# Host-side weight tiles with 8 KB rows, and stored activation sums loaded into a free quarter of a weight buffer

## The chip, the cores and the metric

The kernel runs on one core of a Trainium2 chip. The metric is device time in microseconds (us), lower is better. Engines are named as in the profile: PE is TensorE, DVE is VectorE, ACT is ScalarE, POOL is GpSimd, SP is the sync engine, whose queue issues nearly all DMAs here.

## The reference

One encoder block on a sequence of 256 tokens of width 2048, all in float32:

```python
hn = rmsnorm(h, mix_norm_pre)
proj = hn @ w_in                       # 2048 x 4640: z 1024, xbc 1536, dt 32 and u 1024
y_ssd = ssd_mixer(z, xbc, dt_raw, ...)  # bidirectional Mamba-2 scan
y_pool = pool_mixer(u, pool_w, pool_scale)
mix = concatenate([y_ssd, y_pool]) @ w_out            # 2048 x 2048
h = h + rmsnorm(mix, mix_norm_post)
hn = rmsnorm(h, ffn_norm_pre)
ff = conv_glu(hn, w_ffn_up, ..., w_ffn_down)          # 2048 x 11264, then 5632 x 2048
h = h + rmsnorm(ff, ffn_norm_post)
gate = sigmoid(rmsnorm(h, ple_norm_pre) @ w_ple_gate)  # 2048 x 2048
out = h + rmsnorm(gate * (p @ w_ple), ple_norm_post)   # 256 x 2048
```

## The kernel before

Nearly all the time is matrix products of the 256 tokens with weights that are read from HBM once. To keep float32 accuracy, every operand is split into a high part in a reduced format and a low part, the rest. Each product is then three products: high by high, high by low, low by high. The split of a weight tile is one cast on ACT (names ending in `whi`) and one subtraction on DVE (names ending in `wlo`); it is the function `split`.

Weights come through four buffers of 128 x 2048 float32 (8 KB in each of 128 partitions, 1 MB), all under the tag `raw`; a load takes the next buffer in turn and must wait until the last reader of that buffer is done. SP issues the loads in program order, so a load that waits holds those behind it. The split parts go into five buffers of `whi` and five of `wlo`. Smaller tiles come from a pool of five `mid` buffers. The order of the instructions on each engine is set by the kernel's scheduler, which works from the program and a model of durations.

Four functions load weights. `feature_major` (columns xbc of `w_in`) reads 4 row blocks of 128 x 512, so rows of 2 KB. `feature_pairs` (the up-projection, loads named ug and uv, outputs ga and va) reads 8 blocks of 128 x 256, rows of 1 KB. `token_major` (z, output projection wo, down-projection dn, gate gt, ple) reads two blocks of 128 x 1024, rows of 4 KB, by `pair_of_rows`. A first loop reads the dt and u columns of `w_in` (loads dtur), 128 x 1056 at a time.

In the down-projection the 5632 hidden columns are taken in 22 pairs of 128, and the output columns in two halves of 1024. For 10 of the 22 pairs in the first half and 11 in the second (the list `seven`) the product of 2 x 2 blocks is made with seven products instead of eight (`seven_products`). Such a fast block needs sums of weight quarters (`weight_sums`) and sums of activations. The activation sums are made during the up-projection and stored in HBM, 256 KB for each pair (`block_sums`). `hid_sums` loads them again into a `mid` tile, one block ahead of their use, and splits them into a tile `hs`. The weight sums of 7 pairs are made ahead too, in both halves of the columns, and stored (`block_ahead`); their 14 fast blocks load the sums as one 1 MB tile, `bm`, and of the weights themselves only three quarters, by `three_blocks`, in two pieces: a quarter and a half. The first quarter of that `raw` buffer stays unused. The tiles of a fast block carry its row number: block 5 of the first half is dn010, block 6 is dn012. The output projection has three fast blocks, two of which come through `three_blocks`; their activation sums never leave the chip.

Of the kernel before, what the change touches and what calls it, by code (L numbers as in the profile page):

```python
# [50 lines left out]

def build(nc, a, out):
    x = a["x"][0]
    w_in, w_out, w_up = a["w_in"][0], a["w_out"][0], a["w_ffn_up"][0]
    w_down, w_gate, w_ple = a["w_ffn_down"][0], a["w_ple_gate"][0], a["w_ple"][0]
    out = out[0]

    with tile.TileContext(nc) as tc, \
# [34 lines left out]
        ident = cp.tile([P, P], F32, name="ident")  # L93
        make_identity(nc, ident)

        c_dt = DSSD + 1536
        r0 = wp.tile([P, 2048], F32, tag="raw", bufs=4, name="dtur0")
        for n in range(2):
            first = ins(nc.scalar.dma_start(r0[:, n * 352:(n + 1) * 352],
                                            w_in[:P, c_dt + n * 352:c_dt + (n + 1) * 352]))  # L100

        with tc.issue_after(first):
            nc.scalar.activation(tiny("tables", 1), mhalf[:, 0:1], AF.Exp)
# [32 lines left out]
            return xt[0][:, i:i + 1] if i < V_SCW else vt[:, i - V_SCW:i - V_SCW + 1]  # L136


        spare, ready, held = {}, {}, {}

        def parts(name):

# [16 lines left out]
            last["dma"] = load(r[:, :a_ * b_].rearrange("p (a b) -> p a b", a=a_), src, True)  # L159
            return r  # L160

        def three_blocks(name, w, k0, c0):

            r = wp.tile([P, 2048], F32, tag="raw", bufs=4, name=name)
            load(r[:, 512:1024], w[k0 * P:(k0 + 1) * P, c0 + 512:c0 + 1024], True)
            last["dma"] = load(r[:, 1024:], w[(k0 + 1) * P:(k0 + 2) * P, c0:c0 + 1024], True)
            return r

        class Panel:
# [85 lines left out]
            add(acc[1][1], acc[1][1], s167)  # L255

        def pair_of_rows(w, k0, c0):
            return w[k0 * P:(k0 + 2) * P, c0:c0 + 1024].rearrange("(k p) c -> p k c", p=P), 2, 1024

        def split_two(name, w, k0, c0):  # L260

# [3 lines left out]
        def token_major(name, w, c0, ks, get, acc, tail=1, fast=(), alt=None, sums=None, hooks={}, made=None):  # L265


            group, nu, sums_of = [], len(ks) // 2, {}
            for u in range(nu):
                k0 = ks[2 * u]  # L270
                if u + 1 in fast:
                    sums_of[u + 1] = sums(ks[2 * u + 2])
                if u in fast:
                    sets = made(u, c0)
                    r = three_blocks(f"{name}r{k0}", w, k0, c0) if sets else raw(f"{name}r{k0}", *pair_of_rows(w, k0, c0))
                else:
                    two = ready.pop(name) if u == 0 and name in ready else split_two(name, w, k0, c0)
                if u in hooks:
                    hooks[u]()
                if u in fast:  # L280
                    seven_products(f"{name}{k0}", r, sums_of.pop(u)(), acc, alt, u == fast[0], u == fast[-1],
                                   sets and sets())
                    continue
                group.extend(two)
                if nu - tail <= u < nu - 1:
                    continue

                order = [(t, o, g, q) for t in range(2) for o in columns(acc[t]) for g in group for q in range(3)] \
                    if u == nu - 1 or u - 1 in fast[-1:] else \
                    [(t, o, g, q) for g in group for t in range(2) for q in range(3) for o in columns(acc[t])]  # L290
                for t, (o, c), (k, wh, wl), q in order:
                    xh, xl = (v[:, t * P:(t + 1) * P] for v in get(k))
                    xx, ww = ((xh, wh), (xh, wl), (xl, wh))[q]
                    mm(o, xx, ww[:, c:c + o.shape[-1]], k == ks[0] and q == 0, k == ks[-1] and q == 2)
                if u - 1 in fast[-1:]:
                    combine(name, acc, alt)
                group = []
                aside()

        def feature_major(name, w, c0, get, acc):  # L300

            for u in range(4):
                r = raw(f"{name}r{u}", w[u * 512:(u + 1) * 512, c0:c0 + 512]
                        .rearrange("(k p) c -> p k c", p=P), 4, 512)
                tiles = []

                def step(j, kk, f):
                    k = 4 * u + 2 * j + kk
                    (wh, wl), (xh, xl) = tiles[j], get(k)
                    s = slice(kk * 512 + f * P, kk * 512 + (f + 1) * P)  # L310
                    for q, (ww, xx) in enumerate(((wh, xh), (wh, xl), (wl, xh))):
                        mm(acc[f // 2][:, f % 2 * L:(f % 2 + 1) * L], ww[:, s], xx,
                           k == 0 and q == 0 and f % 2 == 0, k == NK - 1 and q == 2)
# [12 lines left out]
                aside()  # L326

        def feature_pairs(name, w, c0, get, acc):


            def high(u, tiles):
                for j, (wh, _) in enumerate(tiles):
                    for k, f, s in block(u, j):
                        mm(acc[f], wh[:, s], get.both(k), k == 0, False)

            def low(u, tiles):
                for j, (_, wl) in enumerate(tiles):
# [123 lines left out]
        for u in range(0, NK, 2):  # L461
            r = [wp.tile([P, 2048], F32, tag="raw", bufs=4, name=f"dtur{u}") if u else r0, page(f"dtur{u + 1}")]
            for j in range(2):
                k = u + j
                if k == 0:
                    last["dma"] = load(r[0][:, 704:1056], w_in[:P, c_dt + 704:c_dt + 1056])
                    xload(1, 2)
                    x_panel(1, 2)
                    continue
                for c0, c1 in ((0, 704), (704, 1056)) if k == 1 else ((0, 1056),):  # L470
                    last["dma"] = load(r[j][:, c0:c1], w_in[k * P:(k + 1) * P, c_dt + c0:c_dt + c1])
                if k == 1:
                    xload(2, 4)
                elif k in (3, 5, 7):
# [196 lines left out]

        def xbc(slab):
            acc = main(f"xbc{slab}")
            feature_major(f"xb{slab}", w_in, DSSD + slab * 512, hn, acc)
# [90 lines left out]
            [job(mix, 1, 1)],  # L765
        ])
        zacc = [main(f"z{t}") for t in range(2)]
        token_major("z", w_in, 0, list(range(NK)), hn, zacc)
        assert not work


# [56 lines left out]
        def cat_blocks(k):  # L828
# [108 lines left out]
        sums = {u: dp.tile([P, 512], F32, name=f"sums{u}") for u in seven}  # L937
# [21 lines left out]
        def block_sums(u, x):  # L959

            s = mid(f"hs{u}")
            activation_sums(s, x)
            stores.append(lambda: nc.sync.dma_start(sums[u], s[:, :512]))

        def store():
            for st in stores:
# [134 lines left out]
def laid_out(a):  # L1101

    def cols(*vs):
        return np.concatenate([v.reshape(-1, P).T for v in vs], axis=1)

    return {
        "x_cols": np.concatenate([cols(a["mix_norm_pre"][0]),
                                  a["x"][0].T.reshape(NK, P, L).transpose(1, 0, 2).reshape(P, NK * L)], axis=1),
        "p_t": a["p"][0, 0].T.reshape(2, P, L).transpose(1, 0, 2),
# [40 lines left out]
```

## Time and profile before

| | |
|---|---|
| three runs | 1117.62, 1118.17, 1120.74 us; median 1118.17 |
| profiled execution | 1116.37 us; its span is 1114.6 us |
| granted TensorE clock | 0.998 |
| PE / DVE / ACT busy | 99% / 75% / 61% of the span |
| DMA | 275.69 MB, mean 247 GB/s |

"Span" is the time from the first to the last instruction in the profiled execution. "Busy" shares are means over the span. The start of a row in a timeline is in us from the span's start, the next number is its length. A row of the list of waits reads: who waited, for whom, total us, times, longest. In a name, `<-` stands between what is written and what is read; `L87` is line 87 of the kernel.

### The profile page before, as it was taken

The page shows a single profiled execution, that of the slowest core. Times are in us where ns is not written, and L with a number is a line of the kernel's source. Part 1 is how long each engine was busy: PE and PEld are TensorE (multiplying, and loading weights), DVE is VectorE, ACT ScalarE, POOL GpSimd, SP SyncE. Part 2 cuts the span into 40 slices and gives each one's busy share as a digit, 9 for nine tenths or more (in the row PEclk, how much of TensorE's full clock was granted, in tenths as well). Part 3 has the DMA queues.
Part 4 walks back from the last instruction along what each step waited for, and adds up shares of the span by engine and source line. Part 5 has one row for each costly group of instructions (what it writes and reads, how often), then busy time and mean ns, then how long its engine had stood idle before and what let it go on. Part 6 is the DMA issues. An engine that isn't in the chain of part 4 may idle for free.

```text
span 1114.6 us, 15714 instructions
## 1 busy us (share of the span) xinstructions
PE 1102.6 (99%) x6040; PEld 964.0 (86%) x6040; DVE 834.2 (75%) x1047; ACT 683.7 (61%) x1006; POOL 53.0 (5%) x80
## 2 busy tenths in 40 slices
PE   9999999999999999999999999999999999999996
PEld 9999988888788888888888888888888888887885
DVE  6668888879786866767767777676888787897574
ACT  6757876555775565565655655556666466657462
POOL 0300023100200000000000000000000000001001
PEclk9999999999999999999999999999999999999999
DMA  9954445766587977877887797676888789886732
GB/s 354 375 175 150 154 151 186 262 215 224 213 283 252 302 264 247 272 268 255 270 296 254 241 323 255 211 254 205 279 293 303 255 285 314 307 283 214 247 132 76
DMA packets 145739, 275.69 MB, mean 247 GB/s; under 512 B 5504, under 2 KB 98560, under 8 KB 142208
## 3 DMA queue, kind: packets, MB, share of 16 engines
q1 hardware_dynamic: 145376, 274.33, 73.3%
q8 instruction: 47, 0.77, 0.3%
q10 hardware_dynamic: 288, 0.36, 0.1%
q14 instruction: 28, 0.23, 0.1%
HBM read 251.86 MB, written 22.81 MB: 246 GB/s over the span
## 4 chain that ended last, share of the span: by engine, by line
PE 92%; DMA 3%; ACT 2%; issue 1%; DVE 1%; POOL 0%; SPq 0%; DVEq 0%; POOLq 0%; ACTq 0%
PE va L87 22%; PE ga L87 21%; PE dna L87 15%; PE gt L87 7%; PE woa L87 7%; PE xbc L87 6%; PE dns L87 5%; PE z L87 4%; DMA dtur<-w_in 2%; DMA x<-x 1%; PE wos L87 1%; PE yd L87 1%; PE pw L87 1%; PE ple L87 0%; PE seg L87 0%
## 5 line engine op out<-in xcount | busy, mean ns | idle before, releaser
L87 PE MATMUL ga<-wox,ug_0whi 128*128 128x512 f32 x352 | 87.8, 391 | 0.0
L87 PE MATMUL va<-wox,uv_0whi 128*128 128x512 f32 x352 | 87.6, 391 | 0.0
L87 PE MATMUL ga<-wox,ug_1whi 128*128 128x512 f32 x352 | 87.2, 389 | 0.0
L87 PE MATMUL va<-wox,uv_1whi 128*128 128x512 f32 x352 | 86.9, 389 | 0.0
L87 PEld LDWEIGHTS va<-wox,uv_1whi 128*128 128x128 f32 x352 | 66.1, 188 | 13.7
L87 PEld LDWEIGHTS ga<-wox,ug_1whi 128*128 128x128 f32 x352 | 66.0, 188 | 13.7
L87 PEld LDWEIGHTS va<-wox,uv_0whi 128*128 128x128 f32 x352 | 64.6, 188 | 12.5
L87 PEld LDWEIGHTS ga<-wox,ug_0whi 128*128 128x128 f32 x352 | 64.6, 188 | 12.4
L87 PE MATMUL ga<-wox,ug_1wlo 128*128 128x256 f32 x352 | 49.7, 283 | 0.9 <-DVE ug_1wlo L153 0.9
L87 PE MATMUL ga<-wox,ug_0wlo 128*128 128x256 f32 x352 | 49.5, 283 | 0.0
L87 PE MATMUL va<-wox,uv_1wlo 128*128 128x256 f32 x352 | 49.4, 283 | 0.0
L87 PE MATMUL va<-wox,uv_0wlo 128*128 128x256 f32 x352 | 49.2, 283 | 0.0
L87 PEld LDWEIGHTS ga<-wox,ug_0wlo 128*128 128x128 f32 x352 | 46.8, 191 | 1.8
L87 PEld LDWEIGHTS va<-wox,uv_0wlo 128*128 128x128 f32 x352 | 46.7, 191 | 1.7
L87 PEld LDWEIGHTS ga<-wox,ug_1wlo 128*128 128x128 f32 x352 | 45.4, 192 | 1.3 <-DVE ug_1wlo L153 1.3
L87 PEld LDWEIGHTS va<-wox,uv_1wlo 128*128 128x128 f32 x352 | 45.4, 192 | 0.0
L875 POOL TENSOR_SCALAR dnm<-dnq,fmean 128x1 f32<-128x1 f32 x2 | 0.6, 282 | 586.8 <-ACT dnj L872 586.8
L87 PE MATMUL xbc<-hnh,xb_0whi 128*128 128x256 f32 x96 | 27.6, 288 | 0.3 <-ACT u L539 0.3
L87 PE MATMUL xbc<-hnh,xb_1whi 128*128 128x256 f32 x96 | 27.3, 285 | 0.0
L87 PE MATMUL xbc<-hnl,xb_1whi 128*128 128x256 f32 x96 | 27.2, 283 | 0.0
L87 PE MATMUL xbc<-hnh,xb_1wlo 128*128 128x256 f32 x96 | 27.1, 283 | 0.0
L87 PE MATMUL xbc<-hnh,xb_0wlo 128*128 128x256 f32 x96 | 27.1, 283 | 0.0
(1664 smaller groups left out, 3095.6 us busy)
## 6 DMA issues: line engine op xcount, KB each, us to landing
dn0r<-w_ffn_down SPq DMA_DIRECT2D x15, 1024.0 KB, 6.2
dn1r<-w_ffn_down SPq DMA_DIRECT2D x15, 1024.0 KB, 6.9
br<-w_ffn_down SPq DMA_DIRECT2D x14, 1024.0 KB, 5.5
bm<-block SPq DMA_DIRECT2D x14, 1024.0 KB, 5.0
zr<-w_in SPq DMA_DIRECT2D x8, 1024.0 KB, 5.3
wo0r<-w_out SPq DMA_DIRECT2D x8, 1024.0 KB, 5.8
gt0r<-w_ple_gate SPq DMA_DIRECT2D x8, 1024.0 KB, 5.9
gt1r<-w_ple_gate SPq DMA_DIRECT2D x8, 1024.0 KB, 5.5
```

Source lines behind the costliest of these rows:

```text
L87: last["pe"] = ins(nc.tensor.matmul(o, lhsT, rhs, start=start, stop=stop, skip_group_check=True))
L875: nc.gpsimd.tensor_scalar(m, q, 1.0 / D, mean[t], op0=ALU.mult, op1=ALU.add)
```

## The change

The host cuts each weight matrix into the kernel's own tiles before the launch, so that every 1 MB load is one contiguous block with a row of 8 KB in each partition. `w_in` is given as three arrays: z, xbc, and dt with u (there only the row blocks become contiguous, with rows of 4224 bytes as before). In the fast blocks with stored weight sums, the three quarters of weights come in one load instead of two. In the 14 such blocks of the down-projection the stored activation sums are loaded into the first quarter of the same `raw` buffer instead of into a `mid` tile; the 7 other fast blocks keep the old way. The casts and subtractions stay the same in number and size.

```diff
-        def three_blocks(name, w, k0, c0):
+        def three_blocks(name, w, k0, c0, rest=None):
             r = wp.tile([P, 2048], F32, tag="raw", bufs=4, name=name)
-            load(r[:, 512:1024], w[k0 * P:(k0 + 1) * P, c0 + 512:c0 + 1024], True)
-            last["dma"] = load(r[:, 1024:], w[(k0 + 1) * P:(k0 + 2) * P, c0:c0 + 1024], True)
+            if rest is not None:
+                load(r[:, :512], rest, True)
+            last["dma"] = load(r[:, 512:], w[c0 // 1024, k0 // 2][:, 512:], True)
             return r
...
         def pair_of_rows(w, k0, c0):
-            return w[k0 * P:(k0 + 2) * P, c0:c0 + 1024].rearrange("(k p) c -> p k c", p=P), 2, 1024
+            return w[c0 // 1024, k0 // 2].unsqueeze(1), 1, 2048
...
-                if u + 1 in fast:
+                if u + 1 in fast and not made(u + 1, c0):
                     sums_of[u + 1] = sums(ks[2 * u + 2])
                 if u in fast:
                     sets = made(u, c0)
-                    r = three_blocks(f"{name}r{k0}", w, k0, c0) if sets else raw(f"{name}r{k0}", *pair_of_rows(w, k0, c0))
+                    if sets:
+                        r = three_blocks(f"{name}r{k0}", w, k0, c0, stored.get(u) if name[:2] == "dn" else None)
+                        sums_of[u] = sums(k0, r)
+                    else:
+                        r = raw(f"{name}r{k0}", *pair_of_rows(w, k0, c0))
...
-                r = raw(f"{name}r{u}", w[u * 512:(u + 1) * 512, c0:c0 + 512]
-                        .rearrange("(k p) c -> p k c", p=P), 4, 512)
+                r = raw(f"{name}r{u}", w[c0 // 128 + u].unsqueeze(1), 1, 2048)
...
-                r = raw(f"{name}r{u}", w[u * 1024:(u + 1) * 1024, c0:c0 + 256]
-                        .rearrange("(k p) c -> p k c", p=P), 8, 256)
+                r = raw(f"{name}r{u}", w[c0 // 256, u].unsqueeze(1), 1, 2048)
...
-        def hid_sums(k):
-            s = mid(f"sums{k}")
-            load(s[:, :512], sums[k // 2], True)
+        def hid_sums(k, s=None):
+            if s is None:
+                s = mid(f"sums{k}")
+                load(s[:, :512], stored[k // 2], True)
...
+    def tiles(w, kt, n):
+        k, c = w.shape
+        return w.reshape(k // (kt * P), kt, P, c // n, n).transpose(3, 0, 2, 1, 4).reshape(c // n, k // (kt * P), P, kt * n)
...
+        "w_z": tiles(w_in[:, :DSSD], 2, 1024),
+        "w_xb": tiles(w_in[:, DSSD:DSSD + 1536], 4, 512).reshape(12, P, 2048),
+        "w_dtu": w_in[:, DSSD + 1536:].reshape(NK, P, 1056),
+        "w_out": tiles(a["w_out"][0], 2, 1024),
+        "w_ffn_up": tiles(a["w_ffn_up"][0], 8, 256),
+        "w_ffn_down": tiles(a["w_ffn_down"][0], 2, 1024),
```

The order of PE's instructions is the same but for six of them. The orders on SP, ACT and DVE move in the down-projection. SP's queue around the blocks 5 and 6 of the first half, before (`dn0r` is a `raw` buffer; `sums<-sums` loads stored activation sums into a `mid` tile; `bm` is the stored weight sums):

```order
L119 DMA sums_7690<-sums_3039 128x512
L119 DMA dn0r_7728<-w_ffn_down 128x512
L119 DMA dn0r_7728<-w_ffn_down 128x1024
L119 DMA bm_0_7734<-block_0_3050 128x2048
L119 DMA sums_7726<-sums_3040 128x512
L119 DMA dn0r_7773<-w_ffn_down 128x512
L119 DMA dn0r_7773<-w_ffn_down 128x1024
```

and after:

```order
L118 DMA dn0r_7720<-sums_3037 128x512
L118 DMA dn0r_7720<-w_ffn_down 128x1536
L118 DMA bm_0_7726<-block_0_3048 128x2048
L118 DMA dn0r_7765<-sums_3038 128x512
L118 DMA dn0r_7765<-w_ffn_down 128x1536
```

The sums of a block stood ahead of its weight buffer's turn, in a tile of their own; now they are the first thing loaded into that buffer. ACT's casts at the same place, before (`dn06` is block 3, whose sums are in a `mid` tile in both kernels; `hs` is the split of the activation sums; `dn_0` and `dn_1` are the plain block 4):

```order
L152 CAST dn06awhi<-dn0r_7643 128x512
L152 CAST dn06cwhi<-dn06f 128x1024
L152 CAST hs_7731<-sums_7690 128x512
L152 CAST dn06dwhi<-dn06g 128x1024
L152 CAST hs_7776<-sums_7726 128x512
L152 CAST dn_0whi<-dn0r_7692 128x1024
```

and after:

```order
L151 CAST dn06bwhi<-dn0r_7639 128x1024
L151 CAST hs_7723<-dn0r_7720 128x512
L151 CAST dn06awhi<-dn0r_7639 128x512
L151 CAST dn06cwhi<-dn06f 128x1024
L151 CAST dn06dwhi<-dn06g 128x1024
L151 CAST hs_7768<-dn0r_7765 128x512
L151 CAST dn_0whi<-dn0r_7686 128x1024
```

The cast of block 5's sums moved two places up, ahead of dn06awhi; that of block 6 stays ahead of dn_0whi and reads the new buffer.

More of the change, by code (lines that the diff above doesn't have):

```diff
@@ L53, in build @@
     x = a["x"][0]
-    w_in, w_out, w_up = a["w_in"][0], a["w_out"][0], a["w_ffn_up"][0]
-    w_down, w_gate, w_ple = a["w_ffn_down"][0], a["w_ple_gate"][0], a["w_ple"][0]
+    w_out, w_up, w_down, w_gate, w_ple = (a[n] for n in ("w_out", "w_ffn_up", "w_ffn_down", "w_ple_gate", "w_ple"))
+    w_dtu, w_xb, w_z = a["w_dtu"], a["w_xb"], a["w_z"]
     out = out[0]
@@ L94, in build @@
         make_identity(nc, ident)
-        c_dt = DSSD + 1536
         r0 = wp.tile([P, 2048], F32, tag="raw", bufs=4, name="dtur0")
@@ L99, in build @@
             first = ins(nc.scalar.dma_start(r0[:, n * 352:(n + 1) * 352],
-                                            w_in[:P, c_dt + n * 352:c_dt + (n + 1) * 352]))
+                                            w_dtu[0][:, n * 352:(n + 1) * 352]))
         with tc.issue_after(first):
@@ L136, in vec @@
             return xt[0][:, i:i + 1] if i < V_SCW else vt[:, i - V_SCW:i - V_SCW + 1]
-        spare, ready, held = {}, {}, {}
+        spare, ready, held, stored = {}, {}, {}, {}
         def parts(name):
@@ L465, in build @@
                 if k == 0:
-                    last["dma"] = load(r[0][:, 704:1056], w_in[:P, c_dt + 704:c_dt + 1056])
+                    last["dma"] = load(r[0][:, 704:1056], w_dtu[0][:, 704:1056])
                     xload(1, 2)
@@ L470, in build @@
                 for c0, c1 in ((0, 704), (704, 1056)) if k == 1 else ((0, 1056),):
-                    last["dma"] = load(r[j][:, c0:c1], w_in[k * P:(k + 1) * P, c_dt + c0:c_dt + c1])
+                    last["dma"] = load(r[j][:, c0:c1], w_dtu[k][:, c0:c1])
                 if k == 1:
@@ L673, in xbc @@
             acc = main(f"xbc{slab}")
-            feature_major(f"xb{slab}", w_in, DSSD + slab * 512, hn, acc)
+            feature_major(f"xb{slab}", w_xb, slab * 512, hn, acc)
             sc = times_rows(f"xr{slab}", acc, rxb)
@@ L767, in build @@
         zacc = [main(f"z{t}") for t in range(2)]
-        token_major("z", w_in, 0, list(range(NK)), hn, zacc)
+        token_major("z", w_z, 0, list(range(NK)), hn, zacc)
         assert not work
@@ L826, in cat_sums, with cat_blocks @@
             split([cat_s[n][:, c] for n in ("h", "l")], v[:, 512:], 0, 512)
-        def cat_blocks(k):
+        def cat_blocks(k, r=None):
             u = wo_ks.index(k) // 2
@@ L936, in build @@
         seven = [u for u in range(1, 19) if u % 5 in (0, 1, 3)]
-        sums = {u: dp.tile([P, 512], F32, name=f"sums{u}") for u in seven}
+        stored.update({u: dp.tile([P, 512], F32, name=f"sums{u}") for u in seven})
         ahead = [(u, half) for u in seven if u % 5 != 3 for half in range(2)]
@@ L962, in block_sums @@
             activation_sums(s, x)
-            stores.append(lambda: nc.sync.dma_start(sums[u], s[:, :512]))
+            stores.append(lambda: nc.sync.dma_start(stored[u], s[:, :512]))
         def store():
@@ L1104, in cols @@
         return np.concatenate([v.reshape(-1, P).T for v in vs], axis=1)
+    def tiles(w, kt, n):
+        k, c = w.shape
+        return w.reshape(k // (kt * P), kt, P, c // n, n).transpose(3, 0, 2, 1, 4).reshape(c // n, k // (kt * P), P, kt * n)
+    w_in = a["w_in"][0]
     return {
+        "w_z": tiles(w_in[:, :DSSD], 2, 1024),
[4 more added lines that the diff above has]
+        "w_ffn_down": tiles(a["w_ffn_down"][0], 2, 1024),
+        "w_ple_gate": tiles(a["w_ple_gate"][0], 2, 1024),
+        "w_ple": tiles(a["w_ple"][0], 2, 1024),
         "x_cols": np.concatenate([cols(a["mix_norm_pre"][0]),
@@ L1140 @@
     arrays.update(constants())
-    for n in ("p", "mix_norm_pre", "ssd_conv_w", "ssd_conv_b", "ssd_norm", "pool_scale", "ffn_norm_pre",
+    for n in ("p", "w_in", "mix_norm_pre", "ssd_conv_w", "ssd_conv_b", "ssd_norm", "pool_scale", "ffn_norm_pre",
               "ffn_conv_w", "ple_norm_pre", "ffn_conv_b", "ssd_dt_bias", "ssd_a_log", "ssd_d"):
```

## The prediction

> **What bounds the kernel now.** I read the busy shares first, then what TensorE (PE) waits for, then stretches of the span with their DMA share, then the chain. From the page's first and second parts:
>
> ```profile
> PE 1102.6 (99%) x6040; PEld 964.0 (86%) x6040; DVE 834.2 (75%) x1047; ACT 683.7 (61%) x1006; POOL 53.0 (5%) x80
> DMA packets 145739, 275.69 MB, mean 247 GB/s; under 512 B 5504, under 2 KB 98560, under 8 KB 142208
> ```
>
> PE is busy 99%, but its ends are modelled, so a wait can hide inside "busy". The view of waits, for PE alone, is complete in five rows:
>
> ```profile
> PE dtu L108 <- POOL ident masks.py:199: 1.4, 1, 1.4
> PE ga L87 <- DVE ug_1wlo L153: 0.9, 1, 0.9
> PE xbc L87 <- ACT u L539: 0.3, 1, 0.3
> PE dnxt L381 <- DVE h_back L886: 0.3, 1, 0.3
> PE woxt L381 <- DVE h L886: 0.3, 1, 0.3
> ```
>
> Not one of them ends on a load of weights: the first is the warm-up, the other four (1.8 us together) end on VectorE or ScalarE where one stage hands over to the next. Now the two stages that carry most of the loads, the up-projection and the down-projection, with three shorter stretches (columns: stretch and length, PE, PEld, DVE, ACT, POOL busy, clock, DMA share, GB/s):
>
> ```profile
> 303.30:782.80 479.50, 479.50 (x2765) 424.86 (x2766) 345.75 (x429) 281.75 (x419) 3.00 (x3) 1.00 0.80 262
> 782.80:1006.50 223.70, 223.70 (x989) 185.23 (x988) 184.89 (x195) 138.82 (x165) 1.70 (x7) 1.00 0.85 289
> 432.00:459.00 27.00, 27.00 (x161) 24.08 (x160) 18.51 (x22) 15.16 (x26) 0.00 (x0) 1.00 0.67 217
> 459.00:486.00 27.00, 27.00 (x150) 23.63 (x150) 21.19 (x29) 14.73 (x20) 0.00 (x0) 1.00 1.01 325
> 27.00:54.00 27.00, 26.68 (x170) 26.48 (x169) 17.38 (x22) 21.39 (x29) 9.89 (x10) 1.00 1.04 381
> ```
>
> The DMA engines are full in some stretches and a third idle in others, at the full clock, so the question is whether PE feels it. The chain says no:
>
> ```profile
> 427.22 22.23 PE ga L87 x128
> 449.45 22.23 PE va L87 x128
> 471.68 22.23 PE ga L87 x128
> ```
>
> One block of 128 matmuls takes 22.23 us at a DMA share of 0.67 and the same 22.23 us at 1.01. The next starts at the hundredth where the last ended. PE runs its own list of instructions at a fixed rate; loads only have to be there in time. DMA is busy but is not the bound.
>
> **The change, part by part.**
>
> (1) Longer rows. The loads by row size, as they are now (columns: name, count, size, median us from issue to landing):
>
> ```profile
> ug40r<-w_ffn_up SPq DMA_DIRECT2D x2, 1024.0 KB, 6.1
> xb0r<-w_in SPq DMA_DIRECT2D x4, 1024.0 KB, 5.0
> zr<-w_in SPq DMA_DIRECT2D x8, 1024.0 KB, 5.3
> bm<-block SPq DMA_DIRECT2D x14, 1024.0 KB, 5.0
> ug30r<-w_ffn_up SPq DMA_DIRECT2D x2, 1024.0 KB, 5.1
> uv40r<-w_ffn_up SPq DMA_DIRECT2D x2, 1024.0 KB, 10.5
> ```
>
> The first four have rows of 1, 2, 4 and 8 KB, and bm already has the new form: one contiguous tile. 1 MB lands in 5.0 us with 2 KB rows and with 8 KB rows alike; with 1 KB rows it lands in 5.1 us at best and in 10.5 where the stores and reloads of the same stage are in its way (the last two rows). As for throughput, the up-projection moves 262 / 0.80 = 328 GB/s per full DMA share with mostly 1 KB rows, the stretch 27 to 54 moves 381 / 1.04 = 366 with mostly 4 to 8 KB rows. So I estimate that the share of 0.80 falls to about 0.80 x 328 / 366 = 0.72. On the path this is worth nothing, since PE waits for no load. What hides it: the 479.5 us of PE. If that cover were gone, the 0.08 would be 38 us; that is a rival below.
>
> The Trainium skill, "DMA: Bandwidth & Descriptors", section "Why small descriptors are slow (HBM only)", gives a fixed overhead of about 3 cycles per packet against beats of 32 B; worked out from it, an estimate, a 1 KB row costs 35/32 and an 8 KB row 259/256, so 7.5% less DMA time. By that alone the share would be 0.74 and not 0.72; neither changes the sum, but if loads set the pace it would be worth 29 us.
>
> (2) The input projection's rows of 4224 B keep their size and only lie closer together. The start is where PE could feel them. PE's first real matmuls, from the timeline:
>
> ```profile
> 4.93 0.96 PE L87 MATMUL dtu<-dtu0whi,hnh 128*128 128x352 f32 x2
> 8.21 0.48 PE L87 MATMUL dtu<-dtu0whi,hnl 128*128 128x352 f32 x2
> 8.53 0.48 PE L87 MATMUL dtu<-dtu0wlo,hnh 128*128 128x352 f32 x2
> ```
>
> A pair takes 0.32 us once running (8.21 to 8.53). The last row is the ninth pair, so eight pairs took 3.60 us where 2.56 would do: 1.0 us of hidden waiting. The bound is a gain of 1.0 if all of it is the loads, a loss of the same size if landings get that much later; I take 0, because the row size, which is what the DMA engines see, stays.
>
> (3) Fewer issues. Each of the 16 fast blocks with stored weight sums (14 in the down-projection, 2 in the output projection) now takes one load of three quarters instead of two pieces, so 16 issues go from SP's queue. SP waits for buffers most of the time; nothing is gained on the path.
>
> (4) Stored sums into the weight buffer's free quarter, for 14 of the 21 blocks. This is the one place that can hurt, so I work it out at the first pair (blocks 5 and 6, tiles dn010 and dn012). Before, these loads go into their own tile; now each must wait until a weight buffer comes free. SP's issues (L119), ScalarE's casts and VectorE's subtractions there:
>
> ```profile
> 788.71 0.82 SPq L119 DMA_DIRECT2D dn0r<-w_ffn_down  x2
> 792.73 0.38 SPq L119 DMA_DIRECT2D sums<-sums  x1
> 794.05 0.82 SPq L119 DMA_DIRECT2D dn0r<-w_ffn_down  x2
> 790.69 1.05 ACT L152 CAST dn06bwhi<-dn0r 128x1024 fp32r<-128x1024 f32 x1
> 791.73 0.62 ACT L152 CAST dn06awhi<-dn0r 128x512 fp32r<-128x512 f32 x1
> 798.08 0.62 ACT L152 CAST hs<-sums 128x512 fp32r<-128x512 f32 x1 [1.08 <-DMA sums<-sums]
> 798.61 1.05 ACT L152 CAST dn_0whi<-dn0r 128x1024 fp32r<-128x1024 f32 x1
> 793.33 0.69 DVE L153 TENSOR_TENSOR dn06awlo<-dn0r,dn06awhi 128x512 fp32r<-128x512 f32 x1
> 799.69 1.23 DVE L153 TENSOR_TENSOR dn_0wlo<-dn0r,dn_0whi 128x1024 fp32r<-128x1024 f32 x1 [0.26 <-ACT dn_0whi L152]
> 803.09 0.62 PE L87 MATMUL dna<-dn_0whi,hidh 128*128 128x512 f32 x2
> 803.54 0.61 PE L87 MATMUL dna<-dn_0wlo,hidh 128*128 128x512 f32 x2
> ```
>
> and the landings that price it:
>
> ```profile
> dn0r<-w_ffn_down SPq DMA_DIRECT2D x7, 256.0 KB, 4.3
> sums<-sums SPq DMA_DIRECT2D x21, 256.0 KB, 5.4
> ```
>
> The buffer of block 5 is free at 788.71, so its sums go out then. They land 4.3 later at 793.0 (the 256 KB piece that today goes first into that very buffer takes 4.3). In the new order ScalarE's cast of these sums stands between dn06bwhi and dn06awhi. ScalarE, done with dn06bwhi at 791.74, waits until 793.0; the cast ends 0.62 later, dn06awhi at about 794.2, and dn06awlo at 794.9 instead of 794.02. That subtraction frees the buffer for block 6: its sums go out at 794.95 instead of 792.73 and land at 799.25. ScalarE waits for them with dn_0whi queued behind: cast to 799.9, dn_0whi to 800.9 (PE wants it at 803.09), dn_0wlo to 802.2 (PE wants it at 803.54). Cover left: 1.3 us, against 2.6 now (799.69 + 1.23 = 800.92). The cost is 0. With the median of all sums loads, 5.4, twice, everything is 2.2 later and PE waits 0.9. Between 4.3 and 5.4 I take 4.3, since it is the same queue place, size and buffer. A pair like this stands at blocks 5/6, 10/11 and 15/16 in each half: six places, so the upper end is 6 x 0.9 = 5.4 us. The lower end is 0: PE has no wait there to give back.
>
> The Trainium skill, same page, section on latency, puts a DMA at about 2.0 us fixed plus its bytes over 436 GB/s; for 256 KB that is an estimate of 2.6 us. By that figure each landing is 1.7 shorter than I took and nothing in (4) could ever reach PE; the rows above are longer, so they decide.
>
> **Sum.** The profiled execution took 1116.37 us, 1.77 outside its span of 1114.6; the three runs have their median at 1118.17, 1.8 above it. (1) 0, (2) 0, (3) 0, (4) 0: 1116.4 in that frame, 1118.2 against the runs. I forecast 1118.2, no change. About 0.3%, 3.4 us, is what a measurement of this kernel can tell from no change.
>
> **Rivals.**
> - *The sums come late (slower).* Mechanism as in (4): ScalarE's queue is in order, its cast of the stored sums waits for a load that now starts only when a buffer is free, and the casts behind it reach PE too late. For it: ScalarE waits for such loads already, as this row shows (total, times, longest):
>
> ```profile
> ACT hs L152 <- DMA sums<-sums: 11.7, 8, 3.8
> ```
>
>   Against it: the sums are the first and smallest piece in the freed buffer, and the DMA queues get shorter. It decides when the two landings of a pair together exceed 8.6 + 1.3 = 9.9 us. At 5.4 each: 1118.2 + 5.4 = 1123.6.
> - *Loads set the pace after all (faster).* Then 38 us go from the up-projection alone: 1080. For it: shares up to 1.01. Against it: PE's list of waits and the 22.23 us.
> - *Small waits shrink (faster, but not past 0.3%).* If the 1.0 hidden at the start and the 1.8 of the four hand-overs all went: 1118.2 - 2.8 = 1115.4. Against it: the hand-overs end on VectorE and ScalarE, with no load ahead of them.
> - *Rows bring nothing (no change).* The DMA share stays at 0.80 since the packets were long enough; the time is the same 1118.2, by another reason.
>
> **Chances.** Forecast 0.72; rows bring nothing 0.06; small waits shrink 0.05; the sums come late 0.12, nearly all past 0.3%; loads set the pace 0.05. So faster 0.06 (loads, and a little of the small waits), same 0.83, slower 0.11. The range reaches from 1114.8, a little below what all small waits would give, to 1123.6, where the late sums end.
>
> **What would show it.** Right: PE's list of waits has still no load in it; blocks of 22.23 us; packets near 49,000 (each 1 MB load 128 packets instead of 256 to 1024); the up-projection's DMA share near 0.72; ScalarE's waits for stored sums longer in total than 11.7, now on dn0r and dn1r. Wrong by the late sums: new PE waits of about 1 us on VectorE's dn_0wlo or dn_1wlo between 782 and 1006. Wrong by the loads: blocks shorter than 22.23.

## The result

| | before | after |
|---|---|---|
| median of 20 runs each, us | 1118.45 | 1116.43 |
| lowest to highest | 1116.46 to 1121.27 | 1116.08 to 1117.91 |
| runs below 1117.0 | 4 of 20 | 16 of 20 |
| profiled execution / its span | 1116.37 / 1114.6 | 1116.42 / 1114.6 |

The ratio is 0.9983, 95% interval [0.9976, 0.9990]: a gain of 0.17%, 2.0 us in the medians. That is under the 0.3% that the prediction took as the limit of what can be told, but 20 runs on each side tell it. The forecast of no change at 1118.2 was 1.8 us too high.

The two profiled executions have the same span to a tenth of a microsecond. So this gain can't be found by laying one profile beside the other: the lowest times of the two kernels are 0.4 us apart, the highest 3.4 us. What went is the upper part of the spread.

### The profile page after: what moved, and what is told of

Its sections match the earlier page's. It is cut to its first block, busy times and chain, and to the rows that moved or that the text cites. A ratio compares the mean times of both kernels' runs of the same rounds, so it can differ in the third digit from the quotient of the medians.

```text
span 1114.6 us, 15675 instructions
## 1 busy us (share of the span) xinstructions
PE 1102.3 (99%) x6040; PEld 963.5 (86%) x6040; DVE 834.0 (75%) x1047; ACT 685.7 (62%) x1006; POOL 53.0 (5%) x80
## 2 busy tenths in 40 slices
DMA packets 48970, 275.68 MB, mean 247 GB/s; under 512 B 5248, under 2 KB 8192, under 8 KB 21632
## 4 chain that ended last, share of the span: by engine, by line
PE 92%; DMA 3%; ACT 2%; issue 1%; DVE 1%; POOL 0%; SPq 0%; POOLq 0%; DVEq 0%; ACTq 0%
PE va L87 22%; PE ga L87 21%; PE dna L87 15%; PE gt L87 7%; PE woa L87 7%; PE xbc L87 6%; PE dns L87 5%; PE z L87 4%; DMA dtur<-w_dtu 2%; DMA x<-x 1%; PE wos L87 1%; PE yd L87 1%; PE pw L87 1%; PE ple L87 0%; PE seg L87 0%
```

## The profile after

PE's busy time and the number of packets, from the page of the changed kernel:

```profile
PE 1102.3 (99%) x6040; PEld 963.5 (86%) x6040; DVE 834.0 (75%) x1047; ACT 685.7 (62%) x1006; POOL 53.0 (5%) x80
DMA packets 48970, 275.68 MB, mean 247 GB/s; under 512 B 5248, under 2 KB 8192, under 8 KB 21632
```

PE does the same work; the packets fell from 145739 to a third. All of PE's waits in the changed kernel (who, for whom, total, times, longest):

```profile
PE dtu L107 <- POOL ident masks.py:199: 1.4, 1, 1.4
PE ga L87 <- DVE ug_1wlo L152: 0.9, 1, 0.9
PE xbc L87 <- ACT u L541: 0.7, 1, 0.7
PE dnxt L383 <- DVE h_back L888: 0.3, 1, 0.3
PE woxt L383 <- DVE h L888: 0.3, 1, 0.3
```

The same five as before, none ending on a load. The up-projection, the down-projection and a block each of low and high DMA share (columns as before):

```profile
303.30:782.80 479.50, 479.38 (x2764) 424.75 (x2765) 346.01 (x430) 282.17 (x418) 3.16 (x4) 1.00 0.74 263
782.80:1006.50 223.70, 223.70 (x988) 185.23 (x987) 184.53 (x195) 140.56 (x165) 1.67 (x6) 1.00 0.79 289
432.00:459.00 27.00, 27.00 (x162) 24.09 (x161) 18.51 (x22) 15.16 (x26) 0.00 (x0) 1.00 0.61 213
459.00:486.00 27.00, 27.00 (x151) 23.64 (x150) 21.22 (x29) 14.74 (x20) 0.00 (x0) 1.00 0.89 326
```

The DMA share fell from 0.80 to 0.74 and from 0.85 to 0.79 for the same bytes. From the chain:

```profile
427.37 22.23 PE ga L87 x128
449.60 22.23 PE va L87 x128
471.82 22.23 PE ga L87 x128
```

The blocks take 22.23 us as before. And ACT's waits for stored sums:

```profile
ACT hs L151 <- DMA sums<-sums: 2.6, 2, 1.9
ACT hs L151 <- DMA dn0r<-sums: 2.5, 2, 2.1
```

Together 5.1 us where they were 11.7. This is the first line that differs in the direction opposite to the forecast.

## The experiments

Each kernel below is the kernel before with one edit, unless it says otherwise. The table holds what was measured; "below 1117" counts the runs under 1117.0 us. The DMA shares of the two stages and the last column are from each kernel's profiled execution.

The ratios are to runs of the kernel before that were made beside each kernel, so they are not the medians here divided by 1118.45: beside again, layout_only, sums_only and up_only their median was 1117.65 (33 runs), beside dn_only, dn_short and up_tight 1117.73 (23), beside no_sums, hook_late, after_short and up_only2 1117.78 (28); 18 of these 84 runs were under 1117.0.

The last column is a cover: the time from the end of DVE's subtraction dn122cwlo (block 11 of the second half) to PE's first use of it, worked out from two rows of the timeline. 0.05 is what stays between the two rows when PE stands and waits. A PE that is late already widens the cover: its use of dn122cwlo comes 1.6 us later than in the first profile in up_tight, 2.5 in hook_late, 3.1 in dn_short and 5.4 in after_short. At 2.47 and 2.48 no load counts there any more: in these four kernels the cast dn122awhi, which stands just ahead of dn122cwhi on ACT, waits 0.3 us for PE and not for a load.

| kernel | median (lowest to highest), runs | ratio, interval | below 1117 | up share | dn share | cover at dn122cwlo |
|---|---|---|---|---|---|---|
| before, first profile | 1118.45 (1116.46 to 1121.27), 20 | | 4 of 20 | 0.80 | 0.85 | 0.33 |
| again | 1117.96 (1116.07 to 1120.62), 11 | 1.0001 [0.9991, 1.0011] | 4 of 11 | 0.80 | 0.85 | 0.05 |
| again2 | 1117.70, 1 | | 0 of 1 | 0.80 | 0.85 | 0.60 |
| layout_only | 1116.46 (1116.15 to 1117.22), 11 | 0.9989 [0.9980, 0.9998] | 10 of 11 | 0.73 | 0.80 | 2.17 |
| sums_only | 1116.63 (1116.32 to 1118.42), 11 | 0.9991 [0.9982, 0.9999] | 9 of 11 | 0.80 | 0.86 | 2.47 |
| after | 1116.43 (1116.08 to 1117.91), 20 | 0.9983 [0.9976, 0.9990] | 16 of 20 | 0.74 | 0.79 | 2.48 |
| dn_only | 1116.47 (1116.24 to 1119.04), 11 | 0.9989 [0.9981, 0.9998] | 7 of 11 | 0.79 | 0.80 | 1.10 |
| up_only | 1116.70 (1116.20 to 1119.69), 11 | 0.9991 [0.9982, 1.0000] | 9 of 11 | 0.74 | 0.84 | 1.50 |
| up_only2 | 1116.64 (1116.16 to 1119.16), 11 | 0.9998 [0.9989, 1.0008] | 6 of 11 | 0.74 | 0.84 | 1.86 |
| no_sums | 1116.57 (1116.23 to 1116.74), 11 | 0.9985 [0.9976, 0.9994] | 11 of 11 | 0.80 | 0.78 | 2.47 |
| up_tight | 1119.79 (1116.21 to 1121.63), 12 | 1.0014 [1.0004, 1.0025] | 1 of 12 | 0.81 | 0.83 | 0.05 |
| hook_late | 1118.79 (1117.23 to 1121.47), 11 | 1.0012 [1.0003, 1.0021] | 0 of 11 | 0.80 | 0.82 | 2.48 |
| dn_short | 1122.83 (1120.49 to 1124.69), 6 | 1.0040 [1.0027, 1.0054] | 0 of 6 | 0.82 | 0.94 | 0.92 |
| after_short | 1121.37 (1120.97 to 1121.69), 5 | 1.0033 [1.0021, 1.0045] | 0 of 5 | 0.76 | 0.94 | 1.62 |

### again and again2: the kernel before, unchanged

No edit. These are to see what the profile of one execution at 1116.37 doesn't show.

> The kernel before, unchanged, for a second profiled execution and its spread. Theory A (late sums): the stored activation sums reach ScalarE late in the down-projection in most executions; the profile shows a wait of PE of 1 to 4 us in all between 782 and 1006 us that ends on VectorE's hs or on a cast behind it. Theory B (late weights): the waits stand in the up-projection, between 303 and 782 us, behind a load with 1 KB rows. Theory C (the start or the hand-overs): the waits stand before 54 us or at 281 to 303 or 1007 to 1026 us. Time about 1118.4 us, runs from 1116.5 to 1121.

> The kernel before, a third profiled execution. Theory A (a load of stored sums lands too late in the down-projection, ScalarE's casts queue behind it): whatever this execution takes beyond 1116.2 us stands as later starts of PE's blocks between 782 and 1007 us; the blocks of the up-projection stay at 22.23 us. Theory B (late weights in the up-projection): some of it stands between 303 and 782 us.

The profiled execution of again took 1117.96. Laid matmul by matmul over the first profile, PE is 0.1 us behind at 783 us, 0.6 at 954.2, 0.8 at 956 and 1.5 at 1000.4: the loss stands in the down-projection. The first place, in the first profile (start, length; ACT's cast of the sums for a later block, and DVE's subtraction that PE needs; then PE's first use of it):

```profile
942.01 0.39 SPq L119 DMA_DIRECT2D sums<-sums  x1
949.66 0.62 ACT L152 CAST hs<-sums 128x512 fp32r<-128x512 f32 x1 [1.84 <-DMA sums<-sums]
952.04 1.22 DVE L153 TENSOR_TENSOR dn122cwlo<-bm,dn122cwhi 128x1024 fp32r<-128x1024 f32 x1
953.59 0.39 PE L87 MATMUL dns<-dn122cwlo,hs 128*128 128x512 f32 x1
```

The same three rows in the execution of again:

```profile
950.55 0.62 ACT L152 CAST hs<-sums 128x512 fp32r<-128x512 f32 x1 [2.65 <-DMA sums<-sums]
952.94 1.22 DVE L153 TENSOR_TENSOR dn122cwlo<-bm,dn122cwhi 128x1024 fp32r<-128x1024 f32 x1
954.21 0.50 PE L87 MATMUL dns<-dn122cwlo,hs 128*128 128x512 f32 x1 [0.38 <-DVE dn122cwlo L153]
```

and in its chain, the piece that ends at that cast:

```profile
942.82 7.71 DMA sums<-sums
```

A load of 256 KB, issued among 1 MB loads, takes 7.7 us to land. ACT's queue is in order, so dn122awhi and dn122cwhi wait behind the cast of those sums, and DVE's subtraction ends at 954.16. In the first profile it ended at 953.26, and PE wanted it at 953.59. The cover there was 0.33 us, and 0.9 us of lateness used it up. Where the stored sums come late, the kernel before already pays for it.

This place accounts for about half of the 1.5 us. The rest is lost between 997 and 1000 us, where PE waits for DVE's sums of products (L245), and it begins with a load of weights. The weight sum dn136f (block 18), the two sums of products on DVE of which PE waits for the first, and PE's matmul behind it, in the first profile:

```profile
980.00 1.23 DVE L218 TENSOR_TENSOR dn136f<-dn1r 128x1024 f32<-128x1024 f32 x1
998.04 1.29 DVE L245 TENSOR_TENSOR dna<-dna,dn1v 128x512 f32<-128x512 f32 x2
998.93 0.40 PE L87 MATMUL dna<-dn_0whi,hidh__3035 128*128 128x512 f32 x1
```

and in again:

```profile
981.61 1.23 DVE L218 TENSOR_TENSOR dn136f<-dn1r 128x1024 f32<-128x1024 f32 x1 [0.97 <-DMA dn1r<-w_ffn_down]
999.65 1.29 DVE L245 TENSOR_TENSOR dna<-dna,dn1v 128x512 f32<-128x512 f32 x2
1000.40 0.50 PE L87 MATMUL dna<-dn_0whi,hidh__3035 128*128 128x512 f32 x1 [0.21 <-DVE dna L245]
```

dn136f is 1.6 us later, and so are DVE's sums of products 18 us behind it: DVE doesn't catch up in between. The cover at this second place was about 0.2 us in the first profile, less than at dn122cwlo. In the changed kernel dn136f doesn't wait and starts 2.3 us earlier than in the first profile, with PE 0.1 us later at the second place:

```profile
977.70 1.22 DVE L218 TENSOR_TENSOR dn136f<-dn1r 128x1024 f32<-128x1024 f32 x1
```

In again2 the late load is again that of block 18's weights, and the queue that passes it on is DVE's:

```profile
981.39 1.23 DVE L218 TENSOR_TENSOR dn136f<-dn1r 128x1024 f32<-128x1024 f32 x1 [1.52 <-DMA dn1r<-w_ffn_down]
981.47 1.05 ACT L152 CAST dn136bwhi<-dn1r 128x1024 fp32r<-128x1024 f32 x1 [1.91 <-DMA dn1r<-w_ffn_down]
```

dn136f is a weight sum that is made on the spot. Against the first profile both rows, and DVE's work behind them, are 1.4 us late; PE, 0.4 behind ahead of this place, is 1.4 behind at 1004 us, lost at the second place as in again. The 0.4 were lost at 54 us, in the input projection.

### layout_only and sums_only: the two halves of the change

layout_only has all weights in rows of 8 KB, the three quarters in one load, and the sums still in `mid` tiles; sums_only the reverse:

```diff
 layout_only, against the changed kernel:
...
-                        r = three_blocks(f"{name}r{k0}", w, k0, c0, stored.get(u) if name[:2] == "dn" else None)
-                        sums_of[u] = sums(k0, r)
+                        r = three_blocks(f"{name}r{k0}", w, k0, c0)
 sums_only, against the kernel before:
...
+            if rest is not None:
+                load(r[:, :512], rest, True)
             load(r[:, 512:1024], w[k0 * P:(k0 + 1) * P, c0 + 512:c0 + 1024], True)
...
```

> Weights in tiles with 8 KB rows and three quarters in one load, the stored sums still in tiles of their own as before. A (late sums): about 1118.4 us with the spread of before (some 5 us), perhaps a little less since the queues are shorter. B (late weights with short rows): about 1116.4 us, spread under 2 us.

> Weights laid out as before (rows of 1, 2 and 4 KB), the 14 stored sums loaded into the free quarter of the weight buffer. A (late sums): about 1116.4 us, spread under 2 us. B (late weights): about 1118.4 us, spread some 5 us.

Each half alone brings more than half of the gain, 0.9989 and 0.9991. Whether they add up can't be told: their product, 0.9980, lies inside the interval of the whole, 0.9983, and the intervals of both overlap with it as well. Their medians, 1116.46 and 1116.63, lie within 0.2 us of the changed kernel's. Each raises the cover at dn122cwlo above 2 us, by its own way. With longer rows the sums land a little earlier (median of the loads of sums in the down-projection 5.2 us, 5.4 before) and ACT waits 2.0 us for them in that stage instead of 7.9. With the sums in the weight buffer they stand elsewhere in the queue, the median landing of all of them is 4.2, and ACT waits 5.4 us for them in that stage.

### no_sums: the loads of stored sums taken away

The casts named hs read a tile that is on the chip; this leaves out the 21 loads, so the results of the fast blocks are made of other data. The scheduler moves some of these casts and one load of h_back.

```diff
         def hid_sums(k):
-            s = mid(f"sums{k}")
-            load(s[:, :512], sums[k // 2], True)
+            s = hid[0][0].bitcast(F32)
```

> The kernel before without the 21 loads of stored activation sums (5.5 MB): the casts named hs read a tile that is on the chip anyway, so the products of the fast blocks are made of other data. Theory (loads of the down-projection land late in most executions of the kernel before, and ACT's in-order queue passes this on to PE): with no load of sums to wait for and less in the queue, a median of 1116.2 to 1116.7, as in the changed kernel, and few runs above 1117.5. Rival (the weight loads alone are late, the sums are beside the point): 1117.3 to 1118.2, runs up to 1120 as before.

1116.57, and all 11 runs between 1116.23 and 1116.74, the narrowest spread of all kernels here. The rows of the weights are those of before and the DMA share in the up-projection is still

```profile
303.30:782.80 479.50, 479.50 (x2766) 424.89 (x2766) 345.74 (x429) 281.73 (x418) 3.00 (x3) 1.00 0.80 262
782.80:1006.50 223.70, 223.70 (x989) 185.31 (x988) 184.44 (x195) 140.91 (x165) 1.96 (x7) 1.00 0.78 266
```

so a gain doesn't need long rows. What brings it here is either that ACT no longer waits for the sums or that 5.5 MB of transfers are gone; this kernel takes away both and doesn't tell them apart.

### dn_only, up_only, up_only2: one weight matrix at a time

```diff
 dn_only:
...
+            if w is w_down:
+                return w[c0 // 1024, k0 // 2].unsqueeze(1), 1, 2048
...
 up_only, up_only2:
-                r = raw(f"{name}r{u}", w[u * 1024:(u + 1) * 1024, c0:c0 + 256]
-                        .rearrange("(k p) c -> p k c", p=P), 8, 256)
+                r = raw(f"{name}r{u}", w[c0 // 256, u].unsqueeze(1), 1, 2048)
...
```

> Only the down-projection's weights in tiles with 8 KB rows (its rows had 4 KB); same pieces, same order of instructions as before on PE, ScalarE and VectorE. A: the queue ahead of the sums empties sooner, about 1116.6 us, spread under 2 us. B: no change, about 1117.9 us, spread 4 to 5 us.

> Only the up-projection's weights in tiles with 8 KB rows (88 loads, which had rows of 1 KB); all else as before. A (late sums): 1118.4 us as before. B (late weights, 1 KB rows): about 1116.4 us, spread under 2 us. If layout_only is fast and this is not, the rows of 2 and 4 KB (input, output, down, gate) carry it.

> A repetition of the kernel before with only w_ffn_up in 8 KB rows (1116.7 the first time, ratio 0.9991), whose stalls should not depend on the up-projection's rows at all if they arise in the down-projection. If the first result was real: 1116.5 to 1117.0 again, ratio 0.9985 to 0.9993. If it was chance: 1117.4 to 1118.3, ratio 0.9996 to 1.0003.

Rows of 8 KB in `w_ffn_down` alone bring 0.9989: they lower the share in the stage where the stalls are, 0.85 to 0.80, although the 14 blocks with stored weight sums still load their quarters and halves in rows of 2 and 4 KB:

```profile
782.80:1006.50 223.70, 223.70 (x989) 185.23 (x988) 184.48 (x195) 139.51 (x165) 1.75 (x7) 1.00 0.80 288
```

The spread does not fall under 2 us as expected: the runs reach 1119.04, and 4 of 11 stay above 1117.0. Rows of 8 KB in `w_ffn_up` alone came out at 0.9991 once and 0.9998 the second time. The first interval ends at 1.0 and the second holds it, and the runs reach 1119 both times, so the spread of before is still there. The medians, 1116.70 and 1116.64, and 15 of 22 runs under 1117.0, against 18 of 84 of the kernel before, speak for a gain. Whether the up-projection's rows help, and by what way, is not settled.

### up_tight and dn_short: contiguous blocks with short rows

Both have contiguous 1 MB tiles, as the change makes them, but with rows of 1 KB (`w_ffn_up`) or 512 B (`w_ffn_down`):

```diff
 up_tight:
...
+        "w_ffn_up": a["w_ffn_up"][0].reshape(2, 8, P, 44, 256).transpose(3, 0, 1, 2, 4),
 dn_short:
...
+        "w_ffn_down": a["w_ffn_down"][0].reshape(22, 2, P, 2, 8, 128).transpose(3, 0, 1, 4, 2, 5).reshape(2, 22, 16, P, 128),
```

> The up-projection's weights as contiguous 1 MB tiles, but rows of 1 KB as before; same order of instructions. It tells what made up_only quick: if the row length, about 1117.9 us with a spread of 4 to 5 us and an up-projection DMA share of 0.80; if the contiguity, about 1116.7 us. If up_only was chance, 1117.9 us too, and the DMA share alone tells.

> The opposite dose: the down-projection's weights as contiguous 1 MB tiles whose rows have 512 bytes; same order of instructions as before. A with row length as the lever: slower than before, 1119 to 1125 us, PE waits of 2 us or more between 782 and 1007 us on casts behind the stored sums. If it is contiguity and not row length that helps: about 1116.6 us. B: no change, 1117.9 us.

dn_short turns the knob the other way: the share in the down-projection rises to 0.94 and the time to 1122.83.

```profile
782.80:1006.50 223.70, 220.78 (x970) 181.14 (x969) 181.99 (x194) 135.96 (x161) 1.09 (x4) 1.00 0.94 284
```

In its profiled execution (1120.63) PE loses 4.2 us against the first profile of before, all of it in that stage. up_tight shows that contiguous blocks alone bring nothing in the up-projection; it was even slower than before, by 1.4 per thousand, with most of the stalls again in the down-projection, whose loads it doesn't touch. So an edit elsewhere can move the time by as much as one half of the change does, for a reason that is not known. In its profiled execution (1118.52), one of its stalls:

```profile
PE dna L87 <- DVE dn_0wlo L153: 0.7, 1, 0.7
```

and its cause, a weight sum that waits for its weights:

```profile
842.55 1.23 DVE L218 TENSOR_TENSOR dn026f<-dn0r 128x1024 f32<-128x1024 f32 x1 [2.53 <-DMA dn0r<-w_ffn_down]
```

The same row of the first profile of before:

```profile
839.85 1.22 DVE L218 TENSOR_TENSOR dn026f<-dn0r 128x1024 f32<-128x1024 f32 x1 [0.25 <-DMA dn0r<-w_ffn_down]
```

dn026f reads the weights of block 13, and dn_0wlo of block 12, which PE needs first, stands behind it on DVE. The row is 2.7 us later, of which PE's own lag accounts for 0.4. Why these weights land so late here is open.

### hook_late: h_back moved away

The two 1 MB loads of h_back go behind the last load of sums; the scheduler also moves some casts of sums up.

```diff
-            load(t, away[n], True)
+            load(t, away[n], n[0] != "h")
...
-                      hooks={12: lambda: hb.extend(bring_back(f"h{t}") for t in range(2))})
+                      hooks={18: lambda: hb.extend(bring_back(f"h{t}") for t in range(2))})
```

> The kernel before with the two 1 MB loads of h_back moved from around block 11 of the second half to behind the last load of sums; all other loads keep their order, some casts of sums move up. Theory (the tightest place is block 11, where 3.25 MB are issued within 5 us around two loads of sums): the tail goes, median 1116.3 to 1117.0. Rival (lateness is spread over all pairs of fast blocks, h_back is not special): 1117.4 to 1118.2, no change from before. Third way: h_back now collides with the gate's first weights and costs 1 to 3 us at the end of the stage: 1118 to 1121.

The cover at dn122cwlo does go to 2.48, but the time goes up, 1118.79. Its profiled execution (1121.47) has three stalls on dn_0wlo:

```profile
PE dna L87 <- DVE dn_0wlo L153: 2.9, 3, 1.6
```

Against the first profile of before, PE falls back 0.9 us by 54 us, 1.5 us between 828 and 846 us, in the first half, which the edit doesn't touch, 0.7 us at 957 us and 1.9 us by 987 us. At the last place the h_back loads now go out just behind the load of block 18's weights, issued at 975.30. That load takes 8.9 us to land, and the weight sum dn136f waits for it, with dn_0wlo behind it (the second row is from the chain):

```profile
975.74 0.94 SPq L119 DMA_DIRECT2D h_back<-h_away  x2
975.30 8.89 DMA dn1r<-w_ffn_down
984.22 1.22 DVE L218 TENSOR_TENSOR dn136f<-dn1r 128x1024 f32<-128x1024 f32 x1 [3.37 <-DMA dn1r<-w_ffn_down]
```

That the h_back loads slow the load ahead of them is the likely reading, not a measured one. The time lies in the range of the third way that was expected (1118 to 1121), but the collision is with the weights of block 18 and not with the gate's. So block 11 of the second half is neither the only place where loads come late nor, in the first profile, the tightest, and the theory of one place falls. What stays is that loads in the down-projection as a whole land close to their use.

### after_short: the changed kernel with short rows

The changed kernel with `w_ffn_down` laid out as in dn_short.

> The changed kernel, but w_ffn_down comes as contiguous 1 MB tiles with rows of 512 B, so its loads take longer; the stored sums are still in the free quarter of the weight buffer. The same rows in the kernel before gave 1122.8. Theory (sums loaded as the first piece of a freed buffer wait behind less, and stand lateness better): 1118 to 1121. Rival, the prediction's part (4) (two landings of a pair add up, each behind the buffer before it, at six places): as late as the kernel before or later, 1122.8 to 1127.

1121.37 on another chip than dn_short's 1122.83; the two ratios, 1.0033 and 1.0040, overlap. So the new order of the loads of sums stands late loads no better than the old one. Its two stalls are at the operand that part (4) of the prediction named:

```profile
PE dna L87 <- DVE dn_0wlo L152: 4.5, 2, 2.8
```

ACT's waits for stored sums in the down-projection grow to 19.2 us in all, where dn_short has 4.2:

```profile
ACT hs L151 <- DMA dn0r<-sums: 11.2, 6, 3.0
ACT hs L151 <- DMA dn1r<-sums: 4.0, 4, 2.2
ACT hs L151 <- DMA sums<-sums: 4.0, 4, 2.3
```

and the place of the first stall:

```profile
817.90 1.23 DVE L222 TENSOR_TENSOR dn016f<-dn0r 128x1024 f32<-128x1024 f32 x1 [3.50 <-DMA dn0r<-w_ffn_down]
820.32 0.74 PE L87 MATMUL dna<-dn_0wlo,hidh 128*128 128x512 f32 x2 [1.69 <-DVE dn_0wlo L152]
```

The operand (dn_0wlo) is the one foreseen, the cause is not. At 820 the wait ahead of dn_0wlo is that of a weight sum for its weights, not that of ACT for stored sums; the second stall, at 848.6, stands behind dn026f, which waits 4.33 us for its weights. dn_short has its two largest stalls behind the same two weight sums.

## Why the prediction was wrong

**The step that failed** is the sum. It took the 1.8 us between the profiled execution and the median of the runs as a frame, the same for both kernels, and carried it over: 1116.4 becomes 1118.2. The repetitions show that most of these 1.8 us are stalls of PE in the down-projection, which a typical execution of before has and the profiled one has not: again is 1.6 us longer in its span and loses 1.4 of them there, again2 1.3 and 1.0. They were for the change to take away, and it did: the profiled execution of after, at 1116.42, is a typical one of its kernel and has no such stall, and the median of 1116.43 is where the prediction's own frame ended, "1116.4". The sign was on the table: the profiled execution lay below all three runs given, and those reached from 1117.62 to 1120.74. That 1116.43 still lies in the range given is luck: the lower end of 1114.8 stood for waits at the start and at the hand-overs, and the hand-overs stayed (2.2 us in the list after, 1.8 before).

**Part (4), the lower end.** "The lower end is 0: PE has no wait there to give back" was read from the list of waits of that same execution. In again the list has a wait on dn122cwlo of 0.4 us and PE is 1.5 us later at the end of the stage. The two further errors are the place and the direction. The cover was worked out at the first pair of fast blocks, 2.6 us, and taken for six places; at dn122cwlo, in the second half, it was 0.33, and the change raised it to 2.48. And ACT's waits for stored sums, forecast to grow beyond 11.7 us, fell to 5.1.

**What of (4) was right.** At the first pair the chain of waits is the one worked out, in the changed kernel:

```profile
788.73 0.33 SPq L118 DMA_DIRECT2D dn0r<-sums  x1
794.07 0.33 SPq L118 DMA_DIRECT2D dn0r<-sums  x1
799.07 0.62 ACT L151 CAST hs<-dn0r 128x512 fp32r<-128x512 f32 x1 [2.07 <-DMA dn0r<-sums]
800.68 1.23 DVE L152 TENSOR_TENSOR dn_0wlo<-dn0r,dn_0whi 128x1024 fp32r<-128x1024 f32 x1 [0.26 <-ACT dn_0whi L151]
803.69 0.62 PE L87 MATMUL dna<-dn_0wlo,hidh 128*128 128x512 f32 x2
```

The first issue was forecast at 788.71, the second at 794.95, the end of dn_0wlo at 802.2 (it is 1.23 after 800.68, 801.9) and a cover of 1.3 us; it is 1.8, less than the 2.6 of before. The landing taken, 4.3 us, was too long for the first load, which was down when ACT got to it, at most 3.1 us after its issue, and too short for the second, which ACT had to wait for until 5.0 us after its issue; the two errors pull in opposite ways. The rival "the sums come late" names one of the two mechanisms seen, on the wrong kernel. The other, a weight sum on DVE that waits for its weights, stands in none of the rivals. The 2.6 us that (4) sets aside are, in the Trainium skill, "DMA: Bandwidth & Descriptors", section "Anatomy of one DMA — SWDGE (gpsimd) path", a fit for DMAs that POOL issues; SP issues the loads here, and in the kernel before they took 2.6 us at the least and 5.4 in the median.

**Part (1).** Right: 48970 packets (forecast near 49,000), blocks of 22.23 us, no wait for a load in PE's list. The share of the up-projection came out at 0.74, not at the 0.72 of the prediction's estimate. That estimate took its 366 GB/s from the stretch 27 to 54 us as a rate of rows of 4 to 8 KB; the packets there were smaller, 2 KB in the mean:

```profile
DMA packets 5057, 10.30 MB, mean 381 GB/s; under 512 B 216, under 2 KB 2264, under 8 KB 4798
```

0.74 is the figure that the prediction worked out from the Trainium skill, "DMA: Bandwidth & Descriptors", section "Why small descriptors are slow (HBM only)"; the trace of the up-projection agrees with that estimate. The down-projection does not: from rows of 4 KB to rows of 8 KB the same working (131/128 to 259/256) gives 1.1% less, an estimate, and dn_only went from 0.85 to 0.80, 6% less. "On the path this is worth nothing" was wrong for the down-projection: dn_only has 0.9989 and dn_short 1.0040, although the kernel before shows no load in PE's list of waits.

**Parts (2) and (3).** The start can't be told apart: PE's first matmul on dtu1whi begins at 8.2 to 9.0 us in all fourteen traces, at 8.85 before and 8.37 after, and at 8.19 in again, where nothing was changed, and PE's wait for ACT at 54 us is 0.3, 0.7 and 0.6 us in the three executions of the unchanged kernel, and anything up to 1.0 in the others. The 16 issues were not measured alone.

**What stays open.** Why a load lands late in one execution and not in the next, and why up_tight has more stalls in a stage that it doesn't touch. Whether it matters where the arrays of a kernel lie in HBM, no run here tests. What each half of the change is worth, about 1 per thousand, is no larger than the unexplained 1.4 of up_tight. Moving dn016f, dn026f and dn136f behind the subtractions that PE needs first, which would take one of the two ways from a late load to PE, was not tried.

## What to carry to other kernels

Lay the time of the profiled execution beside all runs before using it: if it is among the lowest and the runs spread widely (here over 0.4%), the profile may be of an execution without stalls that the others have, and a list of waits that has no load in it is no proof that loads cost nothing. Then look for the cover, the time from the end of an operand's last preparation to its first use, over the whole stage and not at one place; where it is smaller than the lateness that loads pass on from one execution to the next (here 0.33 us against 0.9, and 0.2 against 1.6), behind an in-order queue that also waits for loads, a lighter DMA can bring time though no wait shows. Take another profile or two of the unchanged kernel first: here two of them, at the usual times of the kernel, showed both places.

## What was not expected of the hardware

- The layout of the weights acts on the DMA share well above rows of 1 KB. For nearly the same bytes the down-projection has 0.94 with 512 B rows in `w_ffn_down`, 0.85 with 4 KB (and 2 KB in the quarters) and 0.80 with 8 KB in the 1 MB loads; the last step also makes these loads contiguous. The up-projection has 0.80 with 1 KB and 0.74 with 8 KB.
- Contiguous blocks with unchanged rows of 1 KB did not lower the share of the up-projection (0.81 against 0.80).
- A 256 KB load takes from 2.6 to 8.3 us to land in one and the same stage. These are the loads of stored sums into their own tiles in the down-projection of the kernel before:

```profile
DMA to landing us min/median/max: 2.6/5.4/8.3
```

After, the 19 loads of stored sums in that stage, 13 of them into a weight buffer and 6 into tiles of their own, land like this:

```profile
DMA to landing us min/median/max: 2.6/3.3/6.2
```
